# Order and pace of the first transfers of a decoder trunk: idle products, x and twelve small weight pieces in turn, late constants

## The chip, the cores and the metric

The kernel runs on one core of one Trainium2 chip. The metric is the device time of one execution in microseconds; lower is better. All times here come from runs and profiles of that one core.

## What is computed

One layer of a decoder trunk over 256 tokens of width 2048, in float32. x is normed, projected by one wide matrix into the queries, keys and values of three attention mixers and their gates, mixed, projected back, and followed by an MLP. Cut to what bears on the start of the kernel:

```python
def reference(x, w_in, ...):
    h = rms_norm(x, norm_mix[layer])
    (a_q, a_kc, a_vc, a_ks, a_vs, a_kw, a_vw, a_gate,
     b_q, b_k, b_v, c_q, c_k, c_v, merge_gate) = jnp.split(h @ w_in[layer], SPLIT_POINTS, axis=-1)
    o_a = nsa_attention(...)
    ...
    x = x + jnp.sum(gate * y, axis=2) @ w_out[layer]
    h = rms_norm(x, norm_mlp[layer])
    x = x + jnp.square(jax.nn.relu(h @ w_mlp_in[layer])) @ w_mlp_out[layer]
    return rms_norm(x, norm_final)
```

## The kernel before

TensorE (PE) does almost all of the work in float32 quality from reduced-precision products: every weight is split into a high part (`hi`, a rounding copy on ScalarE, ACT, line 80) and a low part (`lo`, the difference, on VectorE, DVE, line 81), every activation likewise, and three products are added: hi by hi, hi by lo, lo by hi.

The program is a list of **steps**. Each step is one piece of a weight matrix, mostly 512 KB: it is loaded by a transfer on SP's queue (`load`, line 68) into one of four raw buffers, split by `fetch` (line 73), and multiplied by the step's `mm`. A table of steps is written by functions such as `proj_k`, which calls `dmajor` (line 206) with `cuts`, the borders of the pieces in units of 128 rows of the weight. The main loop at the end of `hybrid_block` walks through the table. At step j it runs the step's `pre` (a callback), advances one of the side tasks (`advance`, line 84), splits piece j+AHEAD (AHEAD is 3), and only then issues the products of piece j. All engines work through their instructions in the order issued, waiting where something is not ready. This order is written out by hand; no scheduler changes it.

The first two projections, "c" and "cv" (compressed keys and values), are mixed piece by piece, with cuts 0, 2, 4, 8, 12, 16: ten pieces, of which 0 to 3 are small (256 KB, eight products each) and 4 to 9 large (512 KB, sixteen products). After them come "s", the queries, and the rest.

x itself (2 MiB) arrives in five transfers between the first weights. A **block** is 256 columns of x: `x_block` (line 155) transposes them with four PE instructions (line 161), and `split_scaled` (line 140) makes the two parts in the tile HT: two scalings on ACT (line 145), then two differences on DVE (line 147). Block i holds rows 256i to 256i+255 of the weight's long side, so that the piece with those rows needs it. In before blocks 0 and 1 come ahead of the loop, and blocks 2 to 7 before steps 1, 2, 4, 5, 6 and 7.

`first_norm` (line 163) is a side task. After eight turns of the loop it squares x in four turns (`squares`, line 666, two ACT instructions at line 669 in each turn), then makes the inverse root (`rs`, lines 171 to 173), a diagonal matrix `diag` from it on DVE (line 177), and from that, with one small PE product `pr` (line 180), a row of factors (line 181). The gain columns for x come from `mix_rows` through another small PE instruction (line 152). Six constants (`rb`, `oh`, `rm`, `cm`, `sink`, `w2`, lines 112 to 123) are asked for on POOL's queue at the very start.

Of the kernel before, what the change touches and what calls it, by code (L numbers as in the profile page):

```python
# [8 lines left out]
F32 = mybir.dt.float32  # L9
# [14 lines left out]
AHEAD = 3  # L24
RAWS = 4
# [9 lines left out]
def hybrid_block(ctx: ExitStack, tc: tile.TileContext, x, w_in, cmp_pos, cmp_w1, cmp_w2, swa_sinks,  # L35
                 w_branch, w_out, w_mlp_in, w_mlp_out, norm_mix, norm_mlp, norm_final, rel_bias,
                 onehot, rmask, cmask, out):
    nc = tc.nc
    big = ctx.enter_context(tc.tile_pool(name="big", bufs=6))
    ring = ctx.enter_context(tc.tile_pool(name="ring", bufs=4))  # L40
    cst = ctx.enter_context(tc.tile_pool(name="cst", bufs=1))
    att = ctx.enter_context(tc.tile_pool(name="att", bufs=1))
# [7 lines left out]
    def bank(name="bank"):  # L50
        return psum.tile([128, 512], F32, name=name, tag="at")

    def obank(name="obank"):
        return psum.tile([128, 512], F32, name=name, tag="o")
# [5 lines left out]
    steps = []  # L60
# [5 lines left out]
    loaded = {}  # L66

    def load(j):
        src, a, b = steps[j][:3]
        loaded[j] = ring.tile([128, a, b], F32, name="raw", tag="raw", bufs=RAWS)  # L70
        nc.sync.dma_start(loaded[j], src)

    def fetch(j):
        if j not in loaded:
            load(j)
        raw = loaded.pop(j)
        a, b = steps[j][1:3]
        hi = ring.tile([128, a, b], F32R, name="hi", tag="hi")
        lo = ring.tile([128, a, b], F32R, name="lo", tag="lo")
        nc.scalar.activation(hi, raw, AF.Copy)  # L80
        nc.vector.tensor_tensor(lo, raw, hi.bitcast(F32), op=OP.subtract)  # L81
        return hi, lo

    def advance():
        while tasks:
            try:
                next(tasks[0][1])
                return
            except StopIteration:
                tasks.pop(0)  # L90
# [8 lines left out]
    def load_x(c0, c1):  # L99
        nc.sync.dma_start(xt[:, :, c0:c1], x[0, :, c0:c1].rearrange("(t p) d -> p t d", p=128))  # L100

    ident = cst.tile([128, 128], F32, name="ident")
    make_identity(nc, ident)
    mix_rows = att.tile([16, 128], F32, name="mix_rows", tag="Lc")
    nc.scalar.dma_start(mix_rows, norm_mix[0].rearrange("(a b) -> a b", b=128))
    rows = att.tile([80, 128], F32, name="rows", tag="P1l")
# [3 lines left out]
    nc.vector.memset(warm, 0.0)  # L110
    nc.scalar.activation(warm, warm, AF.Exp)
    rb = cst.tile([32, 24], F32, name="rb")
    nc.gpsimd.dma_start(rb, rel_bias)
    oh = att.tile([32, NB], F32, name="oh", tag="P0")
    nc.gpsimd.dma_start(oh, onehot)
    rm = att.tile([24, NB], F32, name="rm", tag="hu")
    nc.gpsimd.dma_start(rm, rmask)
    cm = cst.tile([128, 2, 16], F32, name="cm")
    nc.gpsimd.dma_start(cm, cmask)
    sink = cst.tile([128, 8], F32, name="sink")  # L120
    nc.gpsimd.dma_start(sink, swa_sinks.to_broadcast([128, 8]))
    w2 = att.tile([128, 2, 2, 128], F32, name="w2", tag="P1")
    nc.gpsimd.dma_start(w2, cmp_w2[0].rearrange("s (a p) d -> p s a d", p=128))
    nhalf = cst.tile([128, 2], F32, name="nhalf")
    nc.vector.memset(nhalf, -0.5)
    ones = att.tile([128, 128], F32, name="ones", tag="Lc")
# [13 lines left out]
    def split_scaled(tiles, k, src, g0):  # L140

        d = [tiles[(k + a) // 8][:, (k + a) % 8] for a in range(2)]
        g = [gains[:, g0 + k + a:g0 + k + a + 1] for a in range(2)]
        for a in range(2):
            nc.scalar.activation(d[a][:, 0:256], src[:, a], AF.Copy, scale=g[a])
        for a in range(2):
            nc.vector.scalar_tensor_tensor(d[a][:, 256:512], src[:, a], g[a], d[a][:, 0:256].bitcast(F32),
                                           op0=OP.mult, op1=OP.subtract)

    def gain_columns(src, c0, n):  # L150
        pc = obank("pc")
        nc.tensor.transpose(pc[:, 0:n], src, ident[0:n, 0:n])
        nc.vector.tensor_copy(gains[:, c0:c0 + n], pc[:, 0:n])

    def x_block(i):

        b = bank("xT").rearrange("p (a q) -> p a q", a=2)
        for a in range(2):
            k = 2 * i + a
            for tt in range(2):  # L160
                nc.tensor.transpose(b[:, a, tt * 128:(tt + 1) * 128], xt[:, tt, k * 128:(k + 1) * 128], ident)
        split_scaled(HT, 2 * i, b, 0)

    def first_norm():
        for _ in range(8):
            yield
        for c in range(4):
            for tt in range(2):
                squares(xt, tt, c)
            yield  # L170
        nc.vector.tensor_reduce(rs, part, axis=AX.X, op=OP.add)
        nc.vector.tensor_scalar(rs, rs, 1.0 / D, EPS, op0=OP.mult, op1=OP.add)
        nc.gpsimd.tensor_tensor(rs, rs, nhalf, op=OP.pow)
        nc.vector.tensor_scalar(rsh, rs, 0.5, None, op0=OP.mult)
        diag = att.tile([128, 2, 128], F32, name="diag", tag="L0")
        for tt in range(2):
            nc.vector.tensor_scalar(diag[:, tt], ident, rs[:, tt:tt + 1], None, op0=OP.mult)
        yield
        pr = obank("pr")
        nc.tensor.matmul(pr[:, 0:256], ones, diag.rearrange("p t q -> p (t q)"), start=True, stop=True)  # L180
        nc.vector.tensor_copy(rbc, pr[:, 0:256])
        yield
        gain_columns(rows, 16, 80)
# [109 lines left out]
    def proj_k(key, c0, scaled=True, **kw):  # L293
        def ev(ps):
            kT[key] = att.tile([128, 2, 256], F32, name="kv", tag="kv", bufs=4)
            evac_d(kT[key], scaled)(ps)
        dmajor(w, c0, hT, ev, **kw)
# [52 lines left out]
    def load_cmp(n):  # L350

        i, q = divmod(n, 4)
        if q == 0:
            craw[i] = bigt([128, 16, 256], F32, "craw")
        r0 = ((i % 2) * 16 + q * 4) * 128
        nc.sync.dma_start(craw[i][:, q * 4:(q + 1) * 4],
                          cmp_w1[0, i // 2, r0:r0 + 512, :].rearrange("(k p) c -> p k c", p=128))
# [309 lines left out]
    def squares(src, tt, c, n=1):  # L667
        j = att.tile([128, n * 512], F32, name="junk", tag="L1" if n == 2 else "half")
        nc.scalar.activation(j, src[:, tt, c * 512:(c + n) * 512], AF.Square,
                             accum_out=part[:, tt, c:c + 1])  # L670
        if n == 2:
            nc.vector.memset(part[:, tt, c + 1:c + 2], 0.0)
# [119 lines left out]
    def job(f, *a, **kw):  # L792

        n = len(steps)
        f(*a, **kw)
        r = steps[n:]
        del steps[n:]
        return r
# [5 lines left out]
    def before(step, f):  # L804
        g = step[4]
        return step[:4] + ((lambda: (f(), g() if g else None)),) + step[5:]

    def mix(a, b):
        n = max(len(a), len(b))
        r = []  # L810
        for i in range(n):
            r += a[i:i + 1] + b[i:i + 1]
        return r

    cuts = (0, 2, 4, 8, 12, 16)
    c0, c1 = job(proj_k, "c", AKC, False, cuts=cuts), job(proj_k, "cv", AVC, False, cuts=cuts)
    c0[-1] = after(c0[-1], lambda: tasks.append(("X0", build_blocks(0, "c"))))
    c1[-1] = after(c1[-1], lambda: tasks.append(("X1", build_blocks(1, "cv"))))
    steps += mix(c0, c1)
    for i, j in enumerate((1, 2, 4, 5, 6, 7)):  # L820
        steps[j] = before(steps[j], lambda i=i: x_block(i + 2))
    proj_k("s", AKS)
    for g in range(4):
        proj_q(0, AQ, g)
# [2 lines left out]
    n = len(steps)  # L827
    proj_vw()
    for i in range(16):
        j = 9 + 2 * i  # L830
        steps[j] = before(steps[j], lambda i=i: load_cmp(i))
        if i % 4 == 3:
            steps[j + 3] = before(steps[j + 3], lambda i=i: compress(i // 4))
# [26 lines left out]
    n = len(steps)  # L860
    out_proj()
    steps[n + 6] = before(steps[n + 6], lambda: drain("M"))
    n = len(steps)
# [5 lines left out]
    n = len(steps)  # L869
# [2 lines left out]


    ready = {}
    load_x(0, 256)
    load(0)
    load_x(256, 512)
    load(1)
    load_x(512, 1024)
    load(2)  # L880
    load(3)
    load_x(1024, 1536)
    load_x(1536, 2048)
    gain_columns(mix_rows, 0, 16)
    x_block(0)
    ready[0] = fetch(0)
    ready[1] = fetch(1)
    x_block(1)
    ready[2] = fetch(2)
    tasks.append(("N", first_norm()))  # L890
    late = None
    for j in range(len(steps)):
        _, _, _, mm, pre, post = steps[j]
        if pre:
            pre()
        advance()
        if late:
            late()
        for i in range(j + AHEAD, min(j + RAWS - 1, len(steps))):
            if i not in loaded and i not in ready:  # L900
                load(i)
        if j + AHEAD < len(steps):
            ready[j + AHEAD] = fetch(j + AHEAD)
        mm(*ready.pop(j))
        late = post

# [38 lines left out]
```

## Time and profile before

| | us |
|---|---|
| median of 3 runs | 1537.47 |
| lowest and highest of them | 1537.40, 1537.71 |
| the profiled execution's own time | 1539.16 |
| its span | 1537.4 |
| PE busy in the span | 1518.6 |
| DVE busy | 920.6 |
| ACT busy | 701.1 |
| POOL busy | 40.6 |

The span runs from the first to the last instruction of the profiled execution; the rest of its own time lies around it. Busy time of PE comes from modelled ends of pipelined products, so a row's duration for a product is longer than the distance to the next one. Where the text speaks of how long a piece takes, it goes by starts.

### The profile page before, as it was taken

How to read it: one execution, taken by the hardware profiler on the slowest of the kernel's cores; microseconds unless marked ns; L12 is line 12 of the kernel's file. 1: busy time of each engine (PE TensorE's matmuls, PEld its weight loads, DVE VectorE, ACT ScalarE, POOL GpSimd, SP SyncE). 2: the span in 40 equal slices, each digit the busy share in tenths (PEclk: the TensorE clock that was granted, in tenths of full speed). 3: DMA queues.
4: the chain of work that ended last, by engine and by line, in shares of the span. 5: the costliest groups of instructions: out<-in, count | busy, mean ns of one | idle time of the engine just before them, and what ended most of it. 6: DMA issues, size and time to landing. Idle time of an engine off the chain costs nothing.

```text
span 1537.4 us, 20178 instructions
## 1 busy us (share of the span) xinstructions
PE 1518.6 (99%) x7878; PEld 1288.5 (84%) x7878; DVE 920.6 (60%) x1065; ACT 701.1 (46%) x924; POOL 40.6 (3%) x72
## 2 busy tenths in 40 slices
PE   7999999999999999999999999999999999999997
PEld 6888988888898888888888888888888888888885
DVE  5655665665765477447556565655656565555556
ACT  6434455555454455444454443444444343444443
POOL 1001000010000010000000000000000000000002
PEclk9999999999999999999999999999999999999999
DMA  9878556565666665666555656566665656565663
GB/s 279 272 235 219 164 164 174 168 181 172 172 180 188 193 190 164 181 193 229 186 184 179 193 191 193 190 192 189 189 189 189 192 176 205 178 204 180 199 220 115
DMA packets 209951, 294.03 MB, mean 191 GB/s; under 512 B 9888, under 2 KB 129232, under 8 KB 209472
## 3 DMA queue, kind: packets, MB, share of 16 engines
q1 hardware_dynamic: 207504, 287.15, 60.8%
q0 software_dynamic: 2176, 5.20, 1.4%
q8 instruction: 61, 1.00, 0.3%
q10 hardware_dynamic: 176, 0.40, 0.1%
q14 instruction: 34, 0.28, 0.1%
HBM read 290.02 MB, written 2.69 MB: 190 GB/s over the span
## 4 chain that ended last, share of the span: by engine, by line
PE 98%; DMA 1%; DVE 0%; POOL 0%; issue 0%; ACT 0%; POOLq 0%; DVEq 0%; ACTq 0%
PE pair L227 24%; PE pair L252 19%; PE pair L254 19%; PE pair L253 19%; PE pair L225 11%; PE s L445 1%; PE pair L229 1%; PE obank L514 1%; DMA raw<-in_w_in_dram 1%; PE tm L630 0%; PE cps L368 0%; PE s L453 0%; PE pt L491 0%; PE obank L517 0%; PE pt L506 0%
## 5 line engine op out<-in xcount | busy, mean ns | idle before, releaser
L81 DVE TENSOR_TENSOR lo<-raw,hi 128x1024 fp32r<-128x1024 f32 (+2 forms) x526 | 634.9, 1213 | 482.3 <-ACT hi L80 481.1
L80 ACT ACTIVATE hi<-raw 128x1024 fp32r<-128x1024 f32 (+2 forms) x526 | 548.4, 1049 | 617.4 <-PE pair L254 407.6
L227 PE MATMUL pair<-dmaj,hi 128*128 128x512 f32 x1024 | 359.8, 398 | 0.0
L225 PE MATMUL pair<-dmaj,lo 128*128 128x256 f32 x960 | 269.7, 281 | 0.0
L227 PEld LDWEIGHTS pair<-dmaj,hi 128*128 128x128 f32 x1024 | 190.8, 188 | 44.5
L227 PE MATMUL pair<-HT,hi 128*128 128x512 f32 x576 | 205.2, 400 | 0.0
L252 PE MATMUL pair<-hi,hid 128*128 128x512 f32 x496 | 192.9, 389 | 0.0
L253 PE MATMUL pair<-lo,hid 128*128 128x512 f32 x496 | 192.9, 389 | 0.0
L254 PE MATMUL pair<-hi,hid 128*128 128x512 f32 x496 | 192.9, 389 | 0.0
L252 PE MATMUL pair<-hi,HT 128*128 128x512 f32 (+2 forms) x512 | 188.0, 367 | 0.0
L254 PE MATMUL pair<-hi,HT 128*128 128x512 f32 (+2 forms) x512 | 186.1, 364 | 0.0
L253 PE MATMUL pair<-lo,HT 128*128 128x512 f32 (+2 forms) x512 | 185.9, 363 | 0.0
L225 PEld LDWEIGHTS pair<-dmaj,lo 128*128 128x128 f32 x960 | 181.3, 189 | 1.4
L225 PE MATMUL pair<-HT,lo 128*128 128x256 f32 x540 | 153.2, 284 | 3.1 <-DVE lo L81 3.1
L227 PEld LDWEIGHTS pair<-HT,hi 128*128 128x128 f32 x576 | 108.8, 190 | 25.5 <-ACT hi L80 1.5
L254 PEld LDWEIGHTS pair<-hi,hid 128*128 128x128 f32 x496 | 93.1, 188 | 19.5
L253 PEld LDWEIGHTS pair<-lo,hid 128*128 128x128 f32 x496 | 93.1, 188 | 19.3
L254 PEld LDWEIGHTS pair<-hi,HT 128*128 128x128 f32 x512 | 96.5, 188 | 15.1
L252 PEld LDWEIGHTS pair<-hi,hid 128*128 128x128 f32 x496 | 93.1, 188 | 18.9
L252 PEld LDWEIGHTS pair<-hi,HT 128*128 128x128 f32 x512 | 96.5, 189 | 14.8 <-issue 0.7
L253 PEld LDWEIGHTS pair<-lo,HT 128*128 128x128 f32 x512 | 96.6, 189 | 14.7 <-issue 0.2
L225 PEld LDWEIGHTS pair<-HT,lo 128*128 128x128 f32 x540 | 102.6, 190 | 4.5 <-DVE lo L81 3.3
(205 smaller groups left out, 1326.1 us busy)
## 6 DMA issues: line engine op xcount, KB each, us to landing
raw<-in_w_in_dram SPq DMA_DIRECT2D x178, 512.0 KB, 3.8
raw<-in_w_mlp_in_dram SPq DMA_DIRECT2D x128, 512.0 KB, 3.9
raw<-in_w_mlp_out_dram SPq DMA_DIRECT2D x128, 512.0 KB, 4.5
raw<-in_w_branch_dram SPq DMA_DIRECT2D x48, 512.0 KB, 4.3
raw<-in_w_out_dram SPq DMA_DIRECT2D x32, 512.0 KB, 4.5
craw<-in_cmp_w_dram SPq DMA_DIRECT2D x16, 512.0 KB, 5.3
master<-scr POOLq DMA_DIRECT2D x48, 64.0 KB, 3.7
raw<-in_w_in_dram SPq DMA_DIRECT2D x8, 280.0 KB, 5.4
```

The source lines that it names most:

```text
L80: nc.scalar.activation(hi, raw, AF.Copy)
L81: nc.vector.tensor_tensor(lo, raw, hi.bitcast(F32), op=OP.subtract)
L225: nc.tensor.matmul(ps[:, c, 0:256], lo[:, k, cs], r[:, 0:256], start=False, stop=False)
L227: nc.tensor.matmul(ps[:, c, :], hi[:, k, cs], r, start=kt == 0, stop=kt == kts - 1)
L229: nc.tensor.matmul(ps[:, c, 0:256], lo[:, k, cs], r[:, 0:256], start=False, stop=False)
L252: nc.tensor.matmul(o, lh, hi[:, k], start=kt == 0, stop=False)
L253: nc.tensor.matmul(o, lh, lo[:, k], start=False, stop=False)
L254: nc.tensor.matmul(o, ll, hi[:, k], start=False, stop=kt == kts - 1)
L445: nc.tensor.matmul(b[:, h], qp[:, a, 2 * i + h], kp[:, c], start=n == 0, stop=n == 2)
L514: nc.tensor.matmul(ob, v[:, a, 0, g * 128:(g + 1) * 128], P0[c][:, hs], start=first and n == 0, stop=False, skip_group_check=True)
```

## The change

Five things change together.

- Ten idle products of a tile `keep` (filled with ones) by itself, six before the first gain columns, four behind block 0 (`keep_busy`). Nothing reads what they write.
- c and cv are cut at 0, 2, 4, 6, 8, 10, 12, 16: fourteen pieces, of which 0 to 11 are small and 12 and 13 large. For pieces 0 to 3 and 8 to 11 the raw buffer is one of the four that later hold keys (`kv`), so that twelve can be under way.
- x comes in six transfers, and transfers of x and of weights are asked for in turn, in the order of use.
- The loop splits one piece ahead while j is under 11, and three ahead from then on. Only block 0 comes ahead of the loop; block i stands before step 2i-1 for i from 1 to 6, and block 7 with block 6 before step 11.
- The six constants are asked for inside `first_norm`, behind `rs`. The loads of the compression weights (`load_cmp`) begin at step 13 in place of step 9, which is the last step of c and cv in both.

```diff
--- before.py
+++ after.py
@@ -67,7 +67,10 @@
 
     def load(j):
         src, a, b = steps[j][:3]
-        loaded[j] = ring.tile([128, a, b], F32, name="raw", tag="raw", bufs=RAWS)
+        if j < 4 or 8 <= j < 12:
+            loaded[j] = att.tile([128, a, b], F32, name="raw", tag="kv", bufs=4)
+        else:
+            loaded[j] = ring.tile([128, a, b], F32, name="raw", tag="raw", bufs=RAWS)
         nc.sync.dma_start(loaded[j], src)
 
     def fetch(j):
@@ -99,8 +102,16 @@
     def load_x(c0, c1):
         nc.sync.dma_start(xt[:, :, c0:c1], x[0, :, c0:c1].rearrange("(t p) d -> p t d", p=128))
 
+    keep = att.tile([128, 128], F32, name="keep", tag="half")
+    nc.vector.memset(keep, 1.0)
     ident = cst.tile([128, 128], F32, name="ident")
     make_identity(nc, ident)
+
+    def keep_busy(n):
+
+        b = obank("busy")
+        for _ in range(n):
+            nc.tensor.matmul(b[:, 0:128], keep, keep, start=True, stop=True)
     mix_rows = att.tile([16, 128], F32, name="mix_rows", tag="Lc")
     nc.scalar.dma_start(mix_rows, norm_mix[0].rearrange("(a b) -> a b", b=128))
     rows = att.tile([80, 128], F32, name="rows", tag="P1l")
@@ -110,17 +121,19 @@
     nc.vector.memset(warm, 0.0)
     nc.scalar.activation(warm, warm, AF.Exp)
     rb = cst.tile([32, 24], F32, name="rb")
-    nc.gpsimd.dma_start(rb, rel_bias)
     oh = att.tile([32, NB], F32, name="oh", tag="P0")
-    nc.gpsimd.dma_start(oh, onehot)
     rm = att.tile([24, NB], F32, name="rm", tag="hu")
-    nc.gpsimd.dma_start(rm, rmask)
     cm = cst.tile([128, 2, 16], F32, name="cm")
-    nc.gpsimd.dma_start(cm, cmask)
     sink = cst.tile([128, 8], F32, name="sink")
-    nc.gpsimd.dma_start(sink, swa_sinks.to_broadcast([128, 8]))
     w2 = att.tile([128, 2, 2, 128], F32, name="w2", tag="P1")
-    nc.gpsimd.dma_start(w2, cmp_w2[0].rearrange("s (a p) d -> p s a d", p=128))
+
+    def late_constants():
+        nc.gpsimd.dma_start(rb, rel_bias)
+        nc.gpsimd.dma_start(oh, onehot)
+        nc.gpsimd.dma_start(rm, rmask)
+        nc.gpsimd.dma_start(cm, cmask)
+        nc.gpsimd.dma_start(sink, swa_sinks.to_broadcast([128, 8]))
+        nc.gpsimd.dma_start(w2, cmp_w2[0].rearrange("s (a p) d -> p s a d", p=128))
     nhalf = cst.tile([128, 2], F32, name="nhalf")
     nc.vector.memset(nhalf, -0.5)
     ones = att.tile([128, 128], F32, name="ones", tag="Lc")
@@ -171,6 +184,7 @@
         nc.vector.tensor_reduce(rs, part, axis=AX.X, op=OP.add)
         nc.vector.tensor_scalar(rs, rs, 1.0 / D, EPS, op0=OP.mult, op1=OP.add)
         nc.gpsimd.tensor_tensor(rs, rs, nhalf, op=OP.pow)
+        late_constants()
         nc.vector.tensor_scalar(rsh, rs, 0.5, None, op0=OP.mult)
         diag = att.tile([128, 2, 128], F32, name="diag", tag="L0")
         for tt in range(2):
@@ -812,13 +826,13 @@
             r += a[i:i + 1] + b[i:i + 1]
         return r
 
-    cuts = (0, 2, 4, 8, 12, 16)
+    cuts = (0, 2, 4, 6, 8, 10, 12, 16)
     c0, c1 = job(proj_k, "c", AKC, False, cuts=cuts), job(proj_k, "cv", AVC, False, cuts=cuts)
     c0[-1] = after(c0[-1], lambda: tasks.append(("X0", build_blocks(0, "c"))))
     c1[-1] = after(c1[-1], lambda: tasks.append(("X1", build_blocks(1, "cv"))))
     steps += mix(c0, c1)
-    for i, j in enumerate((1, 2, 4, 5, 6, 7)):
-        steps[j] = before(steps[j], lambda i=i: x_block(i + 2))
+    for i, j in enumerate((1, 3, 5, 7, 9, 11, 11)):
+        steps[j] = before(steps[j], lambda i=i: x_block(i + 1))
     proj_k("s", AKS)
     for g in range(4):
         proj_q(0, AQ, g)
@@ -827,7 +841,7 @@
     n = len(steps)
     proj_vw()
     for i in range(16):
-        j = 9 + 2 * i
+        j = 13 + 2 * i
         steps[j] = before(steps[j], lambda i=i: load_cmp(i))
         if i % 4 == 3:
             steps[j + 3] = before(steps[j + 3], lambda i=i: compress(i // 4))
@@ -872,23 +886,22 @@
 
 
     ready = {}
-    load_x(0, 256)
-    load(0)
-    load_x(256, 512)
-    load(1)
-    load_x(512, 1024)
-    load(2)
-    load(3)
+    for k in range(4):
+        load_x(k * 256, (k + 1) * 256)
+        load(2 * k)
+        load(2 * k + 1)
     load_x(1024, 1536)
+    for j in range(8, 12):
+        load(j)
     load_x(1536, 2048)
+    keep_busy(6)
     gain_columns(mix_rows, 0, 16)
     x_block(0)
+    keep_busy(4)
     ready[0] = fetch(0)
-    ready[1] = fetch(1)
-    x_block(1)
-    ready[2] = fetch(2)
     tasks.append(("N", first_norm()))
     late = None
+    done = 1
     for j in range(len(steps)):
         _, _, _, mm, pre, post = steps[j]
         if pre:
@@ -896,11 +909,9 @@
         advance()
         if late:
             late()
-        for i in range(j + AHEAD, min(j + RAWS - 1, len(steps))):
-            if i not in loaded and i not in ready:
-                load(i)
-        if j + AHEAD < len(steps):
-            ready[j + AHEAD] = fetch(j + AHEAD)
+        while done < min(j + (AHEAD if j >= 11 else 1) + 1, len(steps)):
+            ready[done] = fetch(done)
+            done += 1
         mm(*ready.pop(j))
         late = post
```

The order in which ACT works, from the scalings of block 4 to the split of the first large piece that follows the squares; `HT` is x transposed, `junk,part` are the squares of the first norm, `hi` the high part of a piece. Before, from block 4:

```order
L145 ACTIVATE HT1_112<-xT_240,gains_110 128x256 x2
L80 ACTIVATE hi_251<-raw_249 128x1024
L145 ACTIVATE HT1_112<-xT_271,gains_110 128x256 x2
L80 ACTIVATE hi_282<-raw_280 128x1024
L145 ACTIVATE HT1_112<-xT_302,gains_110 128x256 x2
L80 ACTIVATE hi_313<-raw_311 128x1024
L145 ACTIVATE HT1_112<-xT_333,gains_110 128x256 x2
L80 ACTIVATE hi_344<-raw_342 128x1024
L669 ACTIVATE junk_364,part_106<-xt_74 128x512
L669 ACTIVATE junk_366,part_106<-xt_74 128x512
L80 ACTIVATE hi_370<-raw_368 128x1024
```

and with the change, from block 5:

```order
L158 ACTIVATE HT1_108<-xT_324,gains_106 128x256 x2
L683 ACTIVATE junk_333,part_102<-xt_74 128x512
L683 ACTIVATE junk_335,part_102<-xt_74 128x512
L83 ACTIVATE hi_337<-raw_141 128x512
L683 ACTIVATE junk_349,part_102<-xt_74 128x512
L683 ACTIVATE junk_351,part_102<-xt_74 128x512
L83 ACTIVATE hi_353<-raw_143 128x512
L158 ACTIVATE HT1_108<-xT_365,gains_106 128x256 x2
L158 ACTIVATE HT1_108<-xT_374,gains_106 128x256 x2
L683 ACTIVATE junk_383,part_102<-xt_74 128x512
L683 ACTIVATE junk_385,part_102<-xt_74 128x512
L83 ACTIVATE hi_389<-raw_387 128x1024
```

The squares stood between large pieces after all blocks; they now stand in the middle of the blocks, one turn ahead of each of the pieces 9 to 12.

DVE at the start, from the differences of block 1 on; `lo` is the low part of a piece. Before:

```order
L147 SCALAR_TENSOR_TENSOR HT0_111<-xT_153,gains_110,HT0_111 128x256 x2
L81 TENSOR_TENSOR lo_163<-raw_127,hi_162 128x512
L81 TENSOR_TENSOR lo_167<-raw_129,hi_166 128x512
L147 SCALAR_TENSOR_TENSOR HT0_111<-xT_179,gains_110,HT0_111 128x256 x2
L81 TENSOR_TENSOR lo_191<-raw_188,hi_190 128x1024
L147 SCALAR_TENSOR_TENSOR HT0_111<-xT_203,gains_110,HT0_111 128x256 x2
L81 TENSOR_TENSOR lo_215<-raw_212,hi_214 128x1024
L81 TENSOR_TENSOR lo_229<-raw_226,hi_228 128x1024
```

With the change:

```order
L160 SCALAR_TENSOR_TENSOR HT0_107<-xT_187,gains_106,HT0_107 128x256 x2
L84 TENSOR_TENSOR lo_197<-raw_122,hi_196 128x512
L84 TENSOR_TENSOR lo_210<-raw_124,hi_209 128x512
L160 SCALAR_TENSOR_TENSOR HT0_107<-xT_221,gains_106,HT0_107 128x256 x2
L84 TENSOR_TENSOR lo_231<-raw_127,hi_230 128x512
L84 TENSOR_TENSOR lo_243<-raw_129,hi_242 128x512
L160 SCALAR_TENSOR_TENSOR HT0_107<-xT_254,gains_106,HT0_107 128x256 x2
L84 TENSOR_TENSOR lo_264<-raw_132,hi_263 128x512
```

Before, the two lo behind block 1 belong to pieces 2 and 3, and block 2 is first used by piece 4. Now the lo behind block i belong to pieces 2i and 2i+1, which are the ones that use block i. On PE the four transpositions of block i stand between the products of pieces 2i-2 and 2i-1, for i from 1 to 6.

## Rows read from the trace of the kernel before

**Rows 1.** The page, part 1: busy time, share of the span, instructions.

```profile
PE 1518.6 (99%) x7878; PEld 1288.5 (84%) x7878; DVE 920.6 (60%) x1065; ACT 701.1 (46%) x924; POOL 40.6 (3%) x72
```

**Rows 2.** The waits of PE over the span: us in total, times, longest.

```profile
PE pc L152 <- DMA mix_rows<-in_norm_mix_dram: 3.7, 1, 3.7
PE pair L225 <- DVE lo L81: 3.1, 1, 3.1
PE xT L161 <- DMA xt<-in_x_dram: 1.2, 1, 1.2
```

**Rows 3.** Timeline: start, us, engine, line, operation; the mark in projection s.

```profile
38.54 0.28 PE L229 MATMUL pair<-HT,lo 128*128 128x256 f32 x1
```

**Rows 4.** Timeline of the start: block 0, piece 0's first lo and products, block 2.

```profile
4.11 1.11 PE L161 MATMUL xT<-ident,xt 128*128 128x128 f32 x4
...
6.93 0.68 DVE L81 TENSOR_TENSOR lo<-raw,hi 128x512 fp32r<-128x512 f32 x1
...
7.24 0.78 PE L227 MATMUL pair<-HT,hi 128*128 128x512 f32 x1
...
9.82 0.60 PE L161 MATMUL xT<-ident,xt 128*128 128x128 f32 x4
```

**Rows 5.** Timeline of block 6 and of the large piece behind it.

```profile
26.32 0.60 PE L161 MATMUL xT<-ident,xt 128*128 128x128 f32 x4
26.67 0.36 PE L225 MATMUL pair<-HT,lo 128*128 128x256 f32 x1
...
26.95 0.84 ACT L145 ACTIVATE HT<-xT,gains 128x256 fp32r<-128x256 f32 x2 [1.43 <-PE xT L161]
...
27.68 1.06 ACT L80 ACTIVATE hi<-raw 128x1024 fp32r<-128x1024 f32 x1
...
27.82 0.88 DVE L147 SCALAR_TENSOR_TENSOR HT<-xT,gains,HT 128x256 fp32r<-128x256 f32 x2 [1.04 <-ACT HT L145]
...
28.77 1.22 DVE L81 TENSOR_TENSOR lo<-raw,hi 128x1024 fp32r<-128x1024 f32 x1
...
29.54 0.60 PE L161 MATMUL xT<-ident,xt 128*128 128x128 f32 x4
```

**Rows 6.** Timeline of the 3.1 us stop before piece 4.

```profile
16.26 1.06 ACT L80 ACTIVATE hi<-raw 128x1024 fp32r<-128x1024 f32 x1 [2.88 <-DMA raw<-in_w_in_dram]
...
17.34 1.23 DVE L81 TENSOR_TENSOR lo<-raw,hi 128x1024 fp32r<-128x1024 f32 x1 [3.05 <-ACT hi L80]
...
18.62 0.38 PE L225 MATMUL pair<-HT,lo 128*128 128x256 f32 x1 [3.08 <-DVE lo L81]
```

**Rows 7.** Stretches: PE, PEld, DVE, ACT, POOL busy, granted clock, DMA share, GB/s.

```profile
19.50:20.00 0.50, 0.50 (x5) 0.46 (x4) 0.50 (x1) 0.50 (x1) 0.00 (x0) 0.89 0.86 154
20.00:21.00 1.00, 1.00 (x5) 0.81 (x5) 1.00 (x2) 1.00 (x4) 0.00 (x0) 0.50 0.79 227
...
22.50:23.00 0.50, 0.50 (x3) 0.32 (x3) 0.50 (x1) 0.00 (x0) 0.00 (x0) 0.50 0.87 256
23.00:24.00 1.00, 1.00 (x8) 0.95 (x7) 0.54 (x1) 0.27 (x1) 0.00 (x0) 0.85 1.03 353
```

**Rows 8.** The same view, the second 5 us.

```profile
5.00:10.00 5.00, 3.75 (x16) 3.10 (x15) 3.04 (x6) 2.72 (x6) 1.12 (x2) 1.00 1.02 317
```

**Rows 9.** Groups by line and form, first 40 us: busy, mean ns.

```profile
L81 DVE TENSOR_TENSOR lo<-raw,hi 128x512 fp32r<-128x512 f32 x4 | 2.8, 690 | 2.8 <-ACT hi L80 2.8
...
L80 ACT ACTIVATE hi<-raw 128x512 fp32r<-128x512 f32 x4 | 2.5, 631 | 3.4 <-DMA raw<-in_w_in_dram 3.4
```

**Rows 10.** Timeline of ACT: one turn's squares and the hi behind them.

```profile
31.86 0.63 ACT L669 ACTIVATE junk<-xt 128x512 f32<-128x512 f32 x1
...
33.24 1.04 ACT L80 ACTIVATE hi<-raw 128x1024 fp32r<-128x1024 f32 x1
```

**Rows 11.** Timeline of DVE: a lo, and diag behind it.

```profile
42.63 1.23 DVE L81 TENSOR_TENSOR lo<-raw,hi 128x1024 fp32r<-128x1024 f32 x1 [1.09 <-ACT hi L80]
...
45.06 0.48 DVE L177 TENSOR_SCALAR diag<-ident,rs 128x128 f32<-128x128 f32 x2
```

## The prediction

> **What bounds the kernel now.** I read the busy shares first, then the waits of PE over the whole span, then the granted clock in short stretches, and last the timeline of the first 50 us. PE is busy for 1518.6 of 1537.4 us [rows 1], so only what PE waits for, and its clock, can move the end. Beyond a first 3.7 us, in which nothing has arrived, PE has two waits that the view names: 1.2 us for the second piece of x and 3.1 us for a split weight [rows 2]. Both lie in the first 20 us. From 18.62 us on PE runs on to the end of its work, so what the first two projections (the keys "c" and "cv") gain or lose is carried whole to the end. The reader should follow them up to one mark: the second product of the next projection, "s", starts at 38.54 [rows 3]; its first is 0.23 us earlier, at 38.31.
>
> Up to that mark before loses time in three places. First, PE is slow at the start: four transpositions take 1.11 us at 4.11 and 0.60 us at 9.82, and piece 0's eight products fill 7.24 to 9.82 [rows 4], where a later piece of sixteen takes 2.87 us, 26.67 to 29.54, so eight 1.43 [rows 5]. That is 1.2 GHz against 2.4, and of the 1.15 us about 0.15 is the wait for the first lo. Second, the 3.1 us: piece 4 lies behind 1 MiB of x in the queue, so ACT waits for it till 16.26, DVE makes its lo at 17.34 and PE restarts at 18.62 [rows 6]. Third, the clock after that stop: it is granted at 0.50 soon after 19.5 and comes back in 23 to 24 [rows 7]. With 0.50 in every row between, this is about 3.4 us at half speed, or 1.7 us lost.
>
> **What the change removes.** These three: about 1.0 + 3.1 + 1.7 = 5.8 us, if the idle products do hold the clock up and the transfers keep pace. The transfers do: x and all the weights of c and cv are 6.29 MB, and at the 317 GB/s of the second stretch of 5 us [rows 8] they need 19.8 us, so even if nothing had landed by 5 us they would be there at 25. Piece 12 is wanted at about 36 below. The ten idle products cost nothing: the first six lie before 3.7 us, in the first wait [rows 2]; the four behind block 0 take about as long as the four transpositions at the same clock (1.11 us, [rows 4], an estimate), and lie between 5.2 and 7.24 us, where PE waits for the first split. At twice that price they end at 7.4, 0.2 us late. The constants go from the start to behind the first norm, near 40 us; the first use in the program is some dozens of pieces later, under PE's products, so I cost this at nothing.
>
> **What it adds.** The split of piece j+1 is now issued just before the products of piece j, where before it ran three pieces ahead, and block i is transposed before piece 2i-1 and used by piece 2i. ACT and DVE work in the order issued, so the small hi of piece 2i stands behind the two scalings of block i, and its lo behind the two differences. I take the time from block i's first transposition, T, from block 6 of before [rows 5]: transposition 26.32, scalings 26.95 (T+0.63), differences 27.82 (T+1.50), lo 28.77 (T+2.45). A small lo takes 0.69 us [rows 9], and PE starts 0.05 us behind a lo (17.34 + 1.23 against 18.62, [rows 6]): T+3.19. PE itself has 0.35 us of transpositions (26.32 to 26.67) and the 1.43 us of piece 2i-1, and is free at T+1.78. **So PE waits 1.4 us before each of pieces 2, 4, 6 and 8**, 5.6 us in all, and a block follows the last by 3.19 + 1.43 = 4.62 us.
>
> From piece 8 on the squares of the first norm join in: two on each of four turns, 1.38 us of ACT a turn (31.86 to 33.24, [rows 10]). Before, they stood where PE had three pieces in hand. Now each turn stands ahead of the next piece's hi. From T of block 4 = 0:
> - Piece 8 runs 3.19 to 4.62, block 5 starts at 4.62, piece 9 ends at 6.40. ACT scales block 5 at 5.25 to 5.98 (a pair holds ACT 0.73 us, 26.95 to 27.68), squares to 7.36, makes hi 10 by 7.99 (0.63, [rows 9]); lo 10 ends at 8.72. Piece 10 starts at 8.77: **a wait of 2.4 us.**
> - Piece 10 ends at 10.20, blocks 6 and 7 and piece 11 take PE to 12.33. ACT scales both blocks from 10.83 to 12.29, squares to 13.67, makes the large hi 12 by 14.73 (1.06), and DVE lo 12 by 16.00 (1.23). Piece 12 starts at 16.05: **a wait of 3.7 us.**
> - Piece 12 takes 2.87 us ([rows 5]) and ends at 18.92. Next on PE stands the small product with diag. DVE reaches diag only behind lo 13 and lo 14 (18.46), and from the end of a lo to the end of diag it took 1.68 us (43.86 to 45.54, [rows 11]): 20.14. **A wait of 1.3 us.**
> - Piece 13 then ends at 20.19 + 2.87 = 23.06, leaving out two small products that stand behind the mark in before and ahead of it now, and are the same work.
>
> **The sum.** Block 1 starts when piece 0 is done. Piece 0 starts at 7.24 as before; its first lo ends at 6.93 + 0.68 = 7.61 [rows 4], and at full clock the other seven products take about 1.2 us (1.43 less the first): 8.8. Block 4 follows at 8.8 + 3 x 4.62 = 22.66, the mark at 22.66 + 23.06 = 45.7 against 38.3: **7.4 us later.** Waits added (5.6 + 2.4 + 3.7 + 1.3 = 13.0) and block 1's 0.35 us against 5.8 removed give the same within 0.2. One more term is the clock: before lost 1.7 us of it behind a stop of 3.1 us, so I expect the same behind 3.7 us. It makes piece 12 end at 20.6, not 18.9, which swallows the wait for diag and leaves 0.4 us: **+7.8 us**. The profiled execution took 1539.16 us, its span 1537.4 and 1.8 around it; with the change 1547.0. The median shown, 1537.47, is 1.7 below that execution, so the forecast is 1545.3 us.
>
> Bounds: if the start stays at 1.2 GHz, block 1 starts at 9.8, +1.0; if the clock also falls behind the 2.4 us stop, piece 10 takes about 1 us more. If DVE can start on a block when the first of two scalings is done, six chains are 0.4 us shorter, -2.5, and the waits for diag and clock might go too, -1.9. So 1541 to 1547.5 for this case.
>
> **Rivals.**
> - A, the clock falls in every turn (chance 0.11). Before shows one stop of 3.1 us at full clock and the fall behind it; no row shows what 1.4 us in each 4.6 does. At 1.2 GHz a chain has the slow transposition (4.11 to the scalings took 1.15, not 0.63, us in [rows 4]) and a slow piece (about 2.5 against 1.4), +1.6 a turn over four turns, and about 2 more on pieces 10 to 13: +8 to 9, about 1554. [...] Against it: PE still works two thirds of each turn.
> - B, the squares find room (0.07): the last three waits, 7.4 us, go, and only the four chains stay. They balance the gain: 1537.5. The order of issue on ACT speaks against it.
> - C, faster (0.13): **the splits keep ahead of PE.** It decides at one point: if lo 2i is there by T+1.78 rather than T+3.19, for instance since a piece's data let the splits run while PE is on the piece before. Then PE runs from 8.8 through eleven small pieces (15.7), two large ones (5.7) and seven blocks (2.5) to 32.7: 5.6 us sooner, 1531.9. For it speaks that ACT and DVE have under 2.3 us of work for a pair of small pieces and a block, against PE's 3.2; against it, that this work stands in series behind the transposition.
> - D, the idle products do not lift the clock: +1.0, inside the forecast's range.
>
> **How the numbers follow.** Forecast 0.69, A 0.11, B 0.07, C 0.13. A measurement tells 0.2%, about 3.1 us, from no change: forecast and A are slower (0.80), B is the same (0.07), C faster (0.13). The range leaves out B and C: from 1540.5, the forecast's lower bound, to 1552, past its upper bound and into part of A, for clock that falls in some turns.
>
> **What would show it.** Right: waits of PE of about 1.4 us before the lo products of pieces 2, 4, 6 and 8, of 2 to 4 us before pieces 10 and 12, released by DVE's lo; the mark near 46 us; no wait of ACT for weights. Wrong: PE without stops from 9 us on (C), waits of ACT's hi for transfers, products at 0.64 us a pair through the first 30 us (A), or a mark near 38 us.

## The result, and the profile after

| | before | with the change |
|---|---|---|
| median, us | 1537.84 (6 runs) | 1547.71 (6 runs) |
| lowest and highest | 1537.40, 1540.23 | 1546.48, 1548.35 |
| span of the profiled execution | 1537.4 | 1546.4 |
| its own time | 1539.16 | 1548.35 |
| the mark, second product of projection s | 38.54 | 48.18 |

The change makes the kernel slower: the ratio is 1.006, 95% interval 1.005 to 1.0071, 9.9 us by the medians and 9.0 by the spans. The mark moves by 9.6 us, and about 0.6 of these are the two small products (`pr` and `pc`) that before has behind the mark and the change ahead of it. So the 9.0 us are lost by the mark, and what stands behind it takes the same time to within 0.2 us.

First the page's span and busy shares, and the view of PE's waits:

```profile
span 1546.4 us, 20242 instructions
PE 1525.1 (99%) x7898; PEld 1293.4 (84%) x7898; DVE 920.5 (60%) x1070; ACT 701.5 (45%) x928; POOL 40.6 (3%) x72
```

```profile
PE pair L239 <- DVE lo L84: 9.7, 6, 3.4
PE busy L114 <- DVE warm L121: 1.1, 1, 1.1
```

Beside [rows 1] and [rows 2] the reader sees that the 3.1 us for a split are gone and the 1.2 us for x too, and that six waits for a lo, 9.7 us, have come. The view counts from the modelled end of a product, which is about 0.2 us later than the next one could start, so each wait is longer by that in time lost. The start, and the chain of one block (block 2) that answers to [rows 4] and [rows 5]:

```profile
8.38 0.40 PE L241 MATMUL pair<-HT,hi 128*128 128x512 f32 x1
...
8.73 0.40 PE L241 MATMUL pair<-HT,hi 128*128 128x512 f32 x1
8.97 0.60 PE L174 MATMUL xT<-ident,xt 128*128 128x128 f32 x4
...
13.51 0.60 PE L174 MATMUL xT<-ident,xt 128*128 128x128 f32 x4
...
14.15 0.84 ACT L158 ACTIVATE HT<-xT,gains 128x256 fp32r<-128x256 f32 x2 [2.67 <-PE xT L174]
...
15.02 0.88 DVE L160 SCALAR_TENSOR_TENSOR HT<-xT,gains,HT 128x256 fp32r<-128x256 f32 x2 [2.47 <-ACT HT L158]
...
15.82 1.28 DVE L84 TENSOR_TENSOR lo<-raw,hi 128x512 fp32r<-128x512 f32 x2
...
16.55 0.38 PE L239 MATMUL pair<-HT,lo 128*128 128x256 f32 x1 [1.04 <-DVE lo L84]
...
18.06 0.60 PE L174 MATMUL xT<-ident,xt 128*128 128x128 f32 x4
...
22.60 0.60 PE L174 MATMUL xT<-ident,xt 128*128 128x128 f32 x4
```

A pair of products takes 0.35 us already in piece 0, where before took 0.64: the idle products do what they are there for, and piece 0 is done at 8.97, where in before it was at 9.82. The chain of block 2 is scalings at T+0.64, differences at T+1.51, the first lo at T+2.31, and the first product of piece 4 at T+3.04. The next block follows after 4.55 us, the one after (block 4) after 4.54.

Then the turns with the squares, PE's two long waits, the small product and the mark:

```profile
28.51 0.63 ACT L683 ACTIVATE junk<-xt 128x512 f32<-128x512 f32 x1
...
29.89 0.61 ACT L83 ACTIVATE hi<-raw 128x512 fp32r<-128x512 f32 x1
...
31.28 0.58 PE L239 MATMUL pair<-HT,lo 128*128 128x256 f32 x1 [2.15 <-DVE lo L84]
...
36.36 0.65 ACT L683 ACTIVATE junk<-xt 128x512 f32<-128x512 f32 x1
...
37.76 3.88 ACT L83 ACTIVATE hi<-raw 128x1024 fp32r<-128x1024 f32 x4
...
40.11 0.39 PE L239 MATMUL pair<-HT,lo 128*128 128x256 f32 x1 [3.39 <-DVE lo L84]
...
44.35 0.82 PE L194 MATMUL pr<-diag,ones 128*128 128x256 f32 x2
...
48.18 0.28 PE L243 MATMUL pair<-HT,lo 128*128 128x256 f32 x1
```

ACT squares (L683) at 28.51 and reaches hi 10 at 29.89, and again at 36.36 before hi 12 at 37.76. PE waits for the lo behind them till 31.28 and 40.11. The clock, in stretches as in [rows 7] (the granted clock is the third column from the right, the DMA share and GB/s behind it):

```profile
30.00:31.00 1.00, 0.00 (x0) 0.00 (x0) 0.46 (x1) 1.00 (x3) 0.00 (x0) 1.00 0.00 0
31.00:32.00 1.00, 0.72 (x2) 0.71 (x3) 0.23 (x1) 0.97 (x5) 0.00 (x0) 0.58 0.00 0
32.00:33.00 1.00, 1.00 (x5) 0.82 (x4) 0.58 (x1) 0.39 (x1) 0.00 (x0) 0.50 0.00 0
...
34.00:35.00 1.00, 1.00 (x8) 0.99 (x7) 0.00 (x0) 0.08 (x1) 0.00 (x0) 0.72 0.00 0
35.00:36.00 1.00, 1.00 (x9) 0.92 (x8) 0.21 (x1) 1.00 (x3) 0.00 (x0) 1.00 0.00 0
...
40.00:41.00 1.00, 0.89 (x5) 0.80 (x6) 1.00 (x2) 1.00 (x2) 0.00 (x0) 1.00 0.03 8
41.00:42.00 1.00, 1.00 (x6) 0.86 (x5) 1.00 (x2) 0.65 (x1) 0.00 (x0) 0.70 0.71 115
42.00:43.00 1.00, 1.00 (x4) 0.88 (x4) 0.57 (x3) 0.00 (x0) 0.31 (x1) 0.50 1.04 361
...
44.00:45.00 1.00, 1.00 (x5) 0.87 (x4) 1.00 (x2) 0.35 (x1) 1.00 (x3) 0.60 1.00 300
```

It falls to 0.50 twice, at 31.2 and at 41.4, with each of the long waits, and stands there for about 3.4 us each time. The same rows show next to nothing on the transfer queues from 30 to 41 us (8 GB/s in the last row): the weights that had a buffer were there, and the next loads waited for the late splits to free one, as the waits of SP's queue in the first 60 us show:

```profile
SPq L74 <- DVE lo L84: 37.1, 13, 17.4
```

### The profile page after: what moved, and what is told of

The parts are those of the page before. It is cut to its first block, busy times and chain, and to the rows that moved or that the text cites. A ratio compares the mean times of both kernels' runs of the same rounds, so it can differ in the third digit from the quotient of the medians.

```text
span 1546.4 us, 20242 instructions
## 1 busy us (share of the span) xinstructions
PE 1525.1 (99%) x7898; PEld 1293.4 (84%) x7898; DVE 920.5 (60%) x1070; ACT 701.5 (45%) x928; POOL 40.6 (3%) x72
## 4 chain that ended last, share of the span: by engine, by line
PE 97%; DVE 1%; issue 1%; ACT 1%; POOL 0%; DMA 0%; POOLq 0%; DVEq 0%; ACTq 0%
PE pair L241 24%; PE pair L266 19%; PE pair L268 19%; PE pair L267 19%; PE pair L239 11%; PE pair L243 1%; PE s L459 1%; PE obank L528 1%; PE tm L644 0%; PE cps L382 0%; PE s L467 0%; PE pt L505 0%; DVE lo L84 0%; PE obank L531 0%; ACT HT L158 0%
## 5 line engine op out<-in xcount | busy, mean ns | idle before, releaser
L241 PEld LDWEIGHTS pair<-dmaj,hi 128*128 128x128 f32 x1024 | 190.9, 188 | 44.8
```

The source lines that it names most:

```text
L241: nc.tensor.matmul(ps[:, c, :], hi[:, k, cs], r, start=kt == 0, stop=kt == kts - 1)
```

## The experiments

The theory: the cost is that a piece's split is issued one step ahead and a block one piece ahead, with the squares put in the same place, and the clock that the long waits lose. The rivals: the transfers in turn, the fourteen pieces or the late constants cost it; or the idle products do. All times below are medians with the ratio to before in the same job (before there: 1538.64 us, 25 runs, for the first four; 1537.90, 16 runs, for the others). The mark and the span are from the profile; a mark with * has the two small products ahead of it.

| run | us | ratio, interval | span | mark |
|---|---|---|---|---|
| split three ahead | 1539.75 | 1.0006 (0.9997 to 1.0016) | 1537.4 | 39.24* |
| squares later | 1543.89 | 1.0031 (1.0020 to 1.0042) | 1542.0 | 43.63 |
| split and blocks earlier | 1541.05 | 1.0015 (1.0005 to 1.0024) | 1538.2 | 40.27* |
| both | 1534.05 | 0.9971 (0.9959 to 0.9982) | 1532.5 | 33.83 |
| no idle products | 1549.47 | 1.0072 (1.0059 to 1.0084) | 1548.3 | 50.29* |
| idle products in the waits | 1546.43 | 1.0054 (1.0041 to 1.0066) | 1544.8 | 46.33* |
| both, early constants | 1534.32 | 0.9976 (0.9967 to 0.9985) | 1532.0 | 33.64 |
| both, x sooner | 1533.62 | 0.9971 (0.9959 to 0.9982) | 1532.1 | 33.33 |

### The split three pieces ahead

```diff
     ready[0] = fetch(0)
+    ready[1] = fetch(1)
+    ready[2] = fetch(2)
...
-    done = 1
+    done = 3
...
-        while done < min(j + (AHEAD if j >= 11 else 1) + 1, len(steps)):
+        while done < min(j + AHEAD + 1, len(steps)):
```

> The change with one edit: the split runs three pieces ahead from the start, pieces 0 to 2 ahead of the loop; blocks, transfers, idle products and constants as in the change. Theory (late splits): block i still stands one piece before its use, but only its differences are then in the way, so the four waits of 1.4 us fall to 0.7 and the one before piece 10 as well; the one before piece 12 stays near 3.3. 5.5 us less than the change plus some of the clock: 1540.5 to 1542.5. Rival (the transfers in turn, the fourteen pieces or the late constants cost the time): no change, 1547 to 1548. Rival (the idle products cost it): no change either.

It measured 1539.75, 8 us less than the change and not told from before. The fourteen pieces, the order of the transfers, the late constants and the idle products are all still there, so an edit of the splits' issue alone takes back the 8 us (9.0 by the spans), and both rivals fall. It was 0.75 us better than the expected range. Its view of waits and two rows say why:

```profile
PE pair L241 <- DVE HT L160: 2.0, 3, 1.0
PE pair L239 <- ACT HT L158: 1.4, 1, 1.4
```

```profile
10.98 0.50 PE L241 MATMUL pair<-HT,hi 128*128 128x512 f32 x1 [0.18 <-DVE HT L160]
...
12.38 0.60 PE L174 MATMUL xT<-ident,xt 128*128 128x128 f32 x4
```

In a turn PE now waits for the differences (DVE HT, L160) only before the second product of a piece, since the first, with lo, needs only the scaled half of HT. Only one of the four turns shows such a wait in the view, 0.18 us before piece 2. By starts, blocks 1 to 5 stand 3.68, 3.45, 3.44 and 3.44 us apart, where PE without such waits takes 3.22 (the run called both, below): 0.2 to 0.5 us a turn, where 0.7 was expected. The rest of the 2.0 us is 0.86 before the first product of piece 0 and 0.97 before the second of piece 12; the 1.4 us, for ACT, are before the first of piece 12.

### The squares four turns later

```diff
     def first_norm():
-        for _ in range(8):
+        for _ in range(12):
             yield
```

> The change with one edit: the first norm begins four turns later, behind the blocks. Theory: the waits before pieces 2 to 8 stay, the one before piece 10 becomes one more of 1.4 us, the one before piece 12 falls to about 2.5, the one for diag goes: 3.4 us less, and 1 to 2 us more if the clock no longer falls: 1541.5 to 1544.5. Rivals (transfers, idle products): 1547 to 1548. If the four short waits were free and the squares all of it: 1537 to 1539.

It measured 1543.89, inside the theory's range: 3.8 us less than the change. So the squares are part of the cost, and the short waits another: the rival by which the squares are all of it wanted 1537 to 1539. The long wait before piece 10 became one of 1.0 in the view (at 30.18), that before piece 12 one of 2.0, the one for diag went, and the first fall of the clock with them. The clock still fell once, behind the wait before piece 12:

```profile
37.00:38.00 1.00, 1.00 (x6) 0.83 (x5) 1.00 (x2) 0.97 (x4) 0.00 (x0) 0.64 0.71 159
38.00:39.00 1.00, 1.00 (x5) 0.90 (x4) 0.37 (x1) 1.00 (x4) 0.00 (x0) 0.50 1.09 352
...
40.00:41.00 1.00, 1.00 (x6) 0.86 (x5) 0.30 (x1) 0.58 (x3) 0.00 (x0) 0.66 0.92 235
```

### Blocks two pieces earlier, and with the squares later

The first of these adds to the split three ahead

```diff
-    for i, j in enumerate((1, 3, 5, 7, 9, 11, 11)):
-        steps[j] = before(steps[j], lambda i=i: x_block(i + 1))
+    for i, j in enumerate((1, 3, 5, 7, 9, 9)):
+        steps[j] = before(steps[j], lambda i=i: x_block(i + 2))
...
     ready[1] = fetch(1)
+    x_block(1)
     ready[2] = fetch(2)
```

> The change with the split three pieces ahead and each block two pieces earlier (block 1 ahead of the loop); squares as in the change. Theory: no wait before pieces 2 to 10, about 1 us before piece 12 and 2 to 4 us for diag, since the squares still crowd ACT: 1535 to 1538, against 1537.8 of before. Rival transfers: if what arrives late binds, waits of ACT for weights and 1540 or more.

It measured 1541.05, more than expected and 1.3 us more than the one without the earlier blocks; the intervals of these two overlap, and the marks differ by 1.0. The expectation had the waits for lo and diag right. It left out the wait of the transpositions for x, 1.7 us of it for block 1 before piece 0, and the clock behind the wait for diag. What each of the two is worth is not separated. ACT has no wait for weights, which the rival asked for, though its 1540 us or more came. Behind the start PE has no wait to speak of up to piece 12, comes to diag sooner, and waits there:

```profile
PE pr L194 <- DVE diag L191: 3.2, 1, 3.2
PE xT L174 <- DMA xt<-in_x_dram: 2.0, 2, 1.7
PE pair L239 <- DVE lo L84: 0.6, 1, 0.6
```

```profile
34.00:35.00 1.00, 0.00 (x0) 0.00 (x0) 0.59 (x4) 0.41 (x1) 1.00 (x3) 1.00 1.04 359
35.00:36.00 1.00, 0.98 (x4) 0.87 (x5) 1.00 (x1) 0.00 (x0) 1.00 (x3) 0.69 1.09 386
...
37.00:38.00 1.00, 1.00 (x5) 0.89 (x4) 1.00 (x2) 0.00 (x0) 0.78 (x2) 0.50 0.74 151
38.00:39.00 1.00, 1.00 (x6) 0.86 (x5) 0.16 (x1) 0.00 (x0) 0.00 (x0) 0.60 1.09 325
```

The small product with diag starts at 35.02 here and at 35.58 with the blocks late, 0.05 and 0.07 us behind the end of diag: with the squares where they are, ACT and DVE set that point, and earlier blocks gain 0.56 there. Behind the 3.2 us stop the clock is at 0.50 for about 3.4 us, on PE's path, where the other run's fall (31.2 to 34.6) lay ahead of diag, which was not there before 35.51. The second of the two moves the squares four turns later as well.

> As the one with blocks earlier and splits three ahead, and the first norm four turns later. Theory: PE does not wait between piece 0 and projection s: 5.9 us faster than before, 1531 to 1533.5. Rival transfers: slower than that by the waits of ACT for weights, 1536 or more. Rival idle products: 1540 or more.

It measured 1534.05, 0.29% less than before (interval 0.18 to 0.41%): all the parts of the change, with only the order of issue altered, beat both kernels. That is the theory's strongest support. Which of its parts give the 0.3% is not separated here. It came 0.5 us above the expected range, which left out the waits of the transpositions for x:

```profile
PE xT L174 <- DMA xt<-in_x_dram: 1.3, 2, 1.0
PE busy L114 <- DVE warm L121: 1.1, 1, 1.1
```

From piece 0 to projection s PE does not wait otherwise, the pairs stand 0.35 us apart from the first at 8.11, and the granted clock stays at 1.00.

### The change without idle products, and with more of them

```diff
-    keep_busy(6)
     gain_columns(mix_rows, 0, 16)
     x_block(0)
-    keep_busy(4)
```

> The change without its ten idle products. Theory: they lift the clock before piece 0 (its products stood 0.35 us a pair with them, 0.64 in before), so without them block 1 starts about 1 us later and all that follows with it: the mark in projection s at 49.2 instead of 48.2, 1548 to 1549.5 against 1547.7 of the change. Rival (the products cost PE time or delay piece 0): the mark at or before 48.2. Rival (the clock rises by itself by then): no change.

1549.47, as expected, so the ten products are worth something here; the intervals of the two ratios overlap, so the mark (2.1 us later) and the span (1.9 more) carry this, from one profile each. Block 1 starts at 9.85, not 8.97. The mark moved further than expected, by 2.1 us and not 1.0. Piece 1 too stands at 0.64 us a pair for most of its length, so block 2 comes 1.35 us late (14.86 for 13.51). Piece 12 is 1.06 us late (41.17 for 40.11). The other 1.05 us come behind it from the clock, which here is at 0.50 from 40.2 to 47.0, where the change had 41.4 to 44.8:

```profile
40.00:41.00 1.00, 0.00 (x0) 0.00 (x0) 1.00 (x1) 1.00 (x2) 0.00 (x0) 0.60 0.00 0
41.00:42.00 1.00, 0.83 (x3) 0.74 (x4) 1.00 (x2) 1.00 (x2) 0.00 (x0) 0.50 0.00 0
...
45.00:46.00 1.00, 1.00 (x4) 0.81 (x4) 1.00 (x2) 0.00 (x0) 1.00 (x3) 0.50 1.03 315
```

The other way round, the second kernel puts idle products of `ident` by itself into the two long waits:

```diff
+    def fill(n):
+        b = obank("busy")
+        for _ in range(n):
+            nc.tensor.matmul(b[:, 0:128], ident, ident, start=True, stop=True)
+
+    steps[10] = before(steps[10], lambda: fill(8))
+    steps[12] = before(steps[12], lambda: fill(12))
     proj_k("s", AKS)
```

> The change with more idle products, eight ahead of piece 10 and twelve ahead of piece 12, in the two long waits; they need less than the waits at full clock. Theory: the two falls of the clock to half in the change (31.4 to 34.6 and 41.4 to 44.8) go; the first cost about 1.5 us on the chain, of the second the wait for diag gives back 1.3: 1.5 to 2.5 us less than the change, 1545 to 1546.3, with the waits themselves unchanged. Rival (the clock there lies beside ACT and costs nothing): 1547 to 1548. Rival (the products push the pieces back): 1548 or more.

```profile
30.00:35.00 5.00, 4.63 (x33) 4.09 (x32) 2.06 (x4) 3.93 (x11) 0.00 (x0) 1.00 0.00 0
35.00:40.00 5.00, 4.29 (x34) 3.92 (x33) 3.61 (x6) 4.97 (x9) 0.00 (x0) 1.00 0.06 9
40.00:45.00 5.00, 4.02 (x23) 3.29 (x22) 4.12 (x10) 1.82 (x3) 3.78 (x7) 1.00 0.94 294
```

```profile
31.29 0.39 PE L239 MATMUL pair<-HT,lo 128*128 128x256 f32 x1 [0.37 <-DVE lo L84]
...
38.64 0.39 PE L239 MATMUL pair<-HT,lo 128*128 128x256 f32 x1 [0.71 <-DVE lo L84]
...
42.68 0.67 PE L194 MATMUL pr<-diag,ones 128*128 128x256 f32 x2 [0.98 <-DVE diag L191]
...
46.33 0.28 PE L243 MATMUL pair<-HT,lo 128*128 128x256 f32 x1
```

The clock stays at 1.00 and the mark comes at 46.33, 1.85 us sooner, while piece 10 starts at 31.29, as in the change (31.28). So the two falls together cost 1.85 us in these profiles, and the waits themselves stand. The median is 1.3 us less than the change's, just above the expected range, and the intervals of the two ratios overlap. The single executions bear it out: the five with idle products in the waits, all at a mean granted clock of 0.998, took 1546.38 to 1546.70. Of the change's six, the one at 0.998 took 1546.48, and the five at 0.995 to 0.997 took 1547.63 to 1548.35.

### The best order, with early constants, and with x sooner

The first calls `late_constants()` at the start, as before does. The second asks for x and weights in the order x 0, weight 0, x 1, weights 1 to 3, x 2, weights 4 and 5, x 3.

> The fastest so far (blocks earlier, splits three ahead, norm four turns later) with the six constants asked for at the start again, as in before. Theory (transfers alone bind at the start): 0.36 MB more ahead of the second piece of x and what follows, 0.5 to 1.2 us, most of it in waits of the transpositions for x: 1534.5 to 1535.3. Rival (the constants are small and go beside): no change, 1533.8 to 1534.3.

> The fastest so far with the second piece of x asked for ahead of weight piece 1. There block 1 waited 1.0 us for x with PE idle before piece 0. Theory: that wait goes, weight piece 1 is still in time: 0.7 to 1.2 us less, 1532.8 to 1533.4. Rival (piece 0's own split binds piece 0): no change.

1534.32 and 1533.62 against 1534.05: neither is told from the order without it. The constants at the start add to the waits of transpositions for x (2.1 us for 1.3), but piece 0 started sooner in that profile (7.30 for 8.11), and the mark is no later (33.64 for 33.83). That speaks for the rival, that they go beside; but the ratios, 0.9976 and 0.9971, leave room for the 0.5 us or more that I expected, so it stays open. With x sooner the wait for x before piece 0 went from 1.0 to 0.25 us, and piece 0's second product then waited 0.4 us for its lo; the mark is 0.5 us sooner. The ratio is the same, 0.9971, and the median just above the expected range; whether it is a gain stays open at these intervals.

## Why the prediction was right

The time, 1547.71, lies inside the range given, 2.4 us above the forecast and 0.2 us above the forecast's own bounds of 1541 to 1547.5. The range reached further up for rival A, clock lost in some turns. What filled that room was clock lost behind the two long waits, so the mechanism was right, one term was too small, and that the range had the room is in part luck.

**What bounds the kernel** was right: the spans differ by what the mark shows, once the two small products are taken off.

**What the change removes** was right in all three parts. Piece 0's first product came at 6.79, not 7.24, but its second waited for the lo till 7.69, so block 1 started at 8.97 (forecast 8.8). No wait of ACT for weights appears, and the wait before piece 4 for a late transfer is gone. That the transfers keep pace was right too: they stood all but still from 30 to 41 us.

**The four short waits** came as forecast and were put about 0.15 us too large: the chain took 3.04 us and not 3.19, and a wait 1.2 us by starts. The step at fault is a reading: T+2.45 for the lo was taken from a large lo in before, which stood behind its own large hi (27.68 + 1.06 = 28.74, [rows 5]). A small lo follows the differences at T+2.31. A turn took 4.54 us and not 4.62. Block 4 started at 22.60; the forecast was 22.66. That agreement is partly luck: block 1 came 0.17 late, and three turns were 0.08 short each.

**The squares** were right. Piece 10 was put at block 4 + 8.77 and came at 31.28 - 22.60 = 8.68.

**The clock** was the term that was too small. I took one fall, behind the wait before piece 12, swallowed by the one for diag down to 0.4 us, and had a second fall, behind the wait before piece 10, only as a bound of about 1 us. Both came. The first made piece 10 and the transpositions of blocks 6 and 7 slow and moved piece 12 to 40.11, 17.51 behind block 4, where 16.05 was forecast: 1.46 us, all of it carried. That leaves 0.4 us of the 1.85 below for the second, as forecast; so the step that failed is that the first fall was left out of the sum. Without falls, in the run with idle products in the waits, the mark is 46.33; less 0.23 to the first product and about 0.55 for the two small ones that is 45.55, where the replay at full clock gave 45.7. So the sum of waits was right to 0.2 us and the clock cost 1.85 us, not 0.4: 9.1 us in place of 7.8. Two figures in the bounds do not add up, and nothing rests on them: the waits for diag and clock are 1.3 + 0.4 = 1.7, not 1.9, and the lower bound stands once as 1541 and once as 1540.5.

**The rivals.** A, a fall in every turn, did not come: the waits of 1.0 in the view (1.2 by starts) left the clock at 1.00 four times. The Trainium skill, "TensorE: Matmul & The Clock Gate", section "HAM oscillation — how this bites in real kernels", describes a loop that loses the clock in every turn while it waits for its next operand. The Trainium skill draws the waits of that loop as about 3 to 5 us long, so the four short ones here, at 1.00, do not go against it; that the clock fell with a wait of 2.15 us already is this trace's own. B fell with the two long waits. C fell as a forecast, and the experiment with both parts shows what it takes: with the blocks and splits early enough and the squares out of the way, PE runs through at 1534.05. Its price was about 0.9 us optimistic (4.7 us sooner by the mark, not 5.6); the waits for x before piece 0 and before block 2, 1.3 us in the view, cover that. D did not come.

## What to carry to other kernels

Where engines work in issue order, count the chain from the transposition to the product that needs it, and compare it with the work that PE has in between; if the chain is longer, every turn waits, whatever the transfers do. Loading earlier gains only if the split is issued earlier too: the same five edits cost 0.6% with the split one piece ahead, and gained 0.3% with it three ahead, blocks two pieces earlier and the side task moved. A long wait (2.15 and 3.39 us in the change) can cost twice, once by itself and once by the clock behind it; idle products in the wait bought the second back here.

## What the runs showed of the hardware that was not expected

The clock fell with stops of 2.0 and 2.15 us in the view (squares later; the change), shorter than the 3.1 us in before, and stayed through four stops of 1.0 us, one in every 4.5 us. In the run with the split three ahead it fell at 31.2, with stops of 1.39 and 0.97 us that had a single product between them.

How long it stayed low differed: about 3.4 us each time in the change, 6.8 us (40.2 to 47.0) in the run without idle products.

Executions of one kernel differ in it: of the seven with the squares later, three at a mean granted clock of 0.998 took 1542.81 to 1542.93, and four at 0.996 or 0.997 took 1543.89 to 1544.74.

At the start the granted clock is no guide. It reads 1.00 from 5 to 10 us in before [rows 8], while the pairs of piece 0 stand 0.64 us apart, as they do where 0.50 is granted later (32.30 to 32.94 in the change). There the pace has to be read from the starts. By it, the same ten idle products lifted the clock at different times: the four transpositions of block 0 took 1.11 us at 4.14 in the change, and 0.66 at 4.13 in the run with x sooner, whose instructions on PE up to there are the same.
